# Moving two matmul operands by 192 bytes modulo 512 in a two-layer encoder kernel

## The chip, the core and the metric

The kernel runs on one core of a Trainium2 chip. The metric is device time in microseconds (us) of one execution; the time shown is the median of the runs taken, with the lowest and the highest beside it. A profile is one further execution, recorded instruction by instruction.

## What is computed

The reference is a two-layer encoder trunk over 256 tokens of width 2048, in float32. Each layer has an attention part (neighbourhood attention in the first layer, grouped-query attention in the second, both next to cross-attention into 256 memory tokens), an output projection, and a dense MLP with a hidden width of 8192:

```python
for i in range(DEPTH):                       # DEPTH = 2
    n = rms_norm(h, attn_norm[i])
    ...                                      # attention heads, cross-attention
    h = h + jnp.concatenate([mix, cross], axis=-1) @ w_o[i]
    n = rms_norm(h, mlp_norm[i])
    h = h + jnp.square(jax.nn.relu(n @ w_up[i])) @ w_down[i]
return rms_norm(h, final_norm)
```

The change touches the last matrix product of the MLP, with `w_down`.

## The kernel before

**Three products for one.** Matrix products run on TensorE in the type float32r. To keep float32 precision, each operand is split into a high part and a remainder (`split`: ScalarE copies the high part, VectorE subtracts it from the source), and a product is made as high x high, high x low and low x high. In the down product these three matmuls are the lines 1380, 1383 and 1384, in that order.

**A matmul has two operands.** The stationary operand (128 x 128, the weights of TensorE) is loaded first, by an instruction of its own, and the moving operand (128 rows of 256 or 512 columns, 4 bytes each) is then streamed through it. In the up product (`products`, line 419) the parts of `w_up` are stationary and the activations `hT` move, 256 columns at a time. In the down product (`down_grains`) the activations `a_s` are stationary and the parts of `w_down` move, 512 columns at a time.

**The MLP as a sequence of steps.** `add_mlp` writes one order by hand. After four leading up blocks it runs 60 steps per layer; a step is `down[0]`, `up[0]`, `up[1]`, `down[1]`:

- `down[0]` ("first"): nine matmuls with the parts `bh`, `bl` of three column blocks of `w_down`;
- `up[0]` and `up[1]`: 48 matmuls that make the next block of 128 hidden units, with the parts `uh`, `ul`. The first of them uses a separate copy of its weights, `u_0` (in the profile `u`);
- `down[1]` ("second"): twelve matmuls with the parts `th`, `tl` of four *combined* blocks, sums of column blocks that a Strassen scheme of seven products needs.

So twelve matmuls with `th`, `tl` follow the 48 of the up product in each step, and the nine with `bh`, `bl` of the next step follow them. Over both layers there are 120 steps. After the last step some plain down products remain (`plain_grains`); there the rooms of `th` and `tl` are used again for the parts `h_p`, `l_p` of a chunk's second half. In the leading up blocks one half uses the same rooms as `u_th`, `u_tl`.

**The order on the engines.** `run_all` runs the grains in this order and issues preparations a few grains ahead; matmuls of the steps are kept in program order (`pin`). The steps' parts are written by ScalarE (line 516, high part) and VectorE (line 517, remainder).

**Places.** Tiles lie one behind another in each partition of the on-chip memory, so the size of one sets where the next begins. Several constants of the kernel (`U_AT`, `MOVING_AT`, `LAST_AT`, `STILL_AT`, `COPY_AT` and others) shift a tile within a slightly larger room, so that it begins at a chosen byte address modulo 512. "Place" below means byte address modulo 512 in the partition. Worked out from the tile sizes and the order in which the pools stack them, the places in the steps are:

| operand | role | place before | place after |
|---|---|---|---|
| `hT`, chunks 0 to 14 | moving, 256 columns | 160 | 160 |
| `hT`, last chunk (k = 15) | moving, 256 columns | 384 | 384 |
| `uh`, `ul` (two buffers in turn) | stationary | 224 for `up[0]`, 480 for `up[1]` | same |
| `u` (copy of the first weights) | stationary | 352 | 352 |
| `a_s` (all its blocks) | stationary | 128 | 128 |
| `th`, `tl` | moving, 512 columns | 128 | 320 |
| `bh`, `bl` | moving, 512 columns | 128 | 128 |
| `u_th`, `u_tl` (leading up block) | stationary | 224 | 224 |
| `h_p`, `l_p` (plain products) | moving, 512 or 256 columns | 128 | 128 |

Of the kernel before, what the change touches and what calls it, by code (L numbers as in the profile page):

```python
# [11 lines left out]
F32R = mybir.dt.float32r  # L12
# [5 lines left out]
P = 128  # L18
# [15 lines left out]
CH = 2048  # L34
HALF = CH // 2
# [22 lines left out]
U_AT = 96  # L58
# [5 lines left out]
LONGER = {"hi": 128, "lo": 128}  # L64

COPY_AT = 384
MASKED = -1e30


# [95 lines left out]
def encoder_kernel(ctx: ExitStack, tc: tile.TileContext, t: dict, out: bass.AP):  # L165
# [56 lines left out]
    for q in range(4):  # L222
        s = slice(q * 512, (q + 1) * 512)
# [969 lines left out]
    def loaded(src, tag):  # L1193
        raw = at.side.tile([P, CH], F32, tag=tag, bufs=3 if tag == "b" else 2, name=f"raw_{tag}")
        nc.sync.dma_start(raw, src)
        return raw

    def up_grains(layer, m):
        own = {}
        lead = m < LEAD  # L1200

        def load():
            own["raw"] = loaded(t[f"w_up{layer}"][m], "U")

        def prep(hf):

            if m == 2:
                past(lambda: prepared(hf), box["splits"][-1])
                return
            if m == 3 and layer == 0:  # L1210
                past(lambda: prepared(hf), box["ready"])
                return
            if m in (LEAD, LEAD + 1):
                past(lambda: prepared(hf), box["both", m - LEAD])
                return
            if m == 1 and hf == 0 and layer == 0:
                past(lambda: prepared(hf), box["turns"])
                return
            with tc.issue_after(box["summed"].ins) if m == hf == 1 else nullcontext():
                prepared(hf)  # L1220

        def prepared(hf):
            half = 2 * m + hf
            if lead and half in (2, 4, 5, 6, 7):

                if half < 5:
                    room = at.side.tile([P, 2, HALF], F32R, tag="b", bufs=3, name="u_b")
                    own[hf] = room[:, 0], room[:, 1]
                elif half > 5:
                    room = at.mlp.tile([P, 2, HALF], F32R, tag=f"z{hf}", name="u_z")  # L1230
                    own[hf] = room[:, 0], room[:, 1]
                else:
                    s = slice(U_AT // 4, U_AT // 4 + HALF)
                    own[hf] = tuple(at.mlp.tile([P, CH], F32R, tag=x, name=f"u_{x}")[:, s] for x in ("th", "tl"))
                box["splits"].append(split(*own[hf], own["raw"][:, hf * HALF : (hf + 1) * HALF]))
            else:
                own[hf] = half_of_side(own["raw"], hf)
            if not lead and hf == 0:

                room = at.side.tile([P, 256], F32R, tag="junk", bufs=1, name="u_0")  # L1240
                own["first"] = room[:, COPY_AT // 4 :][:, :P]
                nc.scalar.activation(own["first"], own["raw"][:, :P], AF.Copy)

        def run(hf):
            if m == hf == 0:
                closed("cat", "ring")
                at.mlp = opened("mlp")

                last = at.mlp.tile([P, 14 * P], F32R, tag="a", bufs=6, name="hT_l")[:, LAST_COPY_AT // 4 :][:, :SEQ]
                nc.scalar.activation(last, box["hT"][:, KT - 1, :SEQ].bitcast(F32), AF.Copy)  # L1250
                box["hT0"] = Plain(box["hT"], last)
            if hf == 0:
                if lead:
                    pool, tag, bufs = (at.att, "att", at.banks) if m == 2 else (at.acc, "acc", None)
                    own["ps"] = pool.tile([P, 512], F32, tag=tag, bufs=bufs, name="ps_u")[:, :SEQ]
                else:
                    own["ps"] = sum_of("up")[:, :SEQ]

            acts = box["hT0" if lead else "hT"]
            if m < 3 and hf == 1:  # L1260
                hi, lo = own.pop(hf)
                last = products(own["ps"], acts, KT // 2, KT // 4, hi, lo)
                box.setdefault("rests", []).append((m, own["ps"], hi[:, HALF // 2 :], lo[:, HALF // 2 :]))
                if m == 2:
                    for other, ps, hi, lo in box.pop("rests"):
                        with tc.issue_after(last.ins):
                            last = products(ps, acts, KT * 3 // 4, KT // 4, hi, lo)
                        squared(layer, other, ps)
                return
            with tc.issue_after(box["late"].ins) if m == hf == 0 else nullcontext():  # L1270
                products(own["ps"], acts, hf * (KT // 2), KT // 2, *own.pop(hf),
                         keep_order=not lead, first=own.pop("first", None))

        def after():
            if m > 2:
                squared(layer, m, own["ps"])

        early = (8, 8, 6)
        return [Grain(lambda: run(0), None, load, None, lambda: prep(0), early if m < 2 else SOONER),
                Grain(lambda: run(1), after, None, None, lambda: prep(1), early if m == 0 else SOONER)]  # L1280
# [44 lines left out]
    def down_grains(layer, n, begins, ends, sooner):  # L1325

        q, j = STEPS[n]
        own = {}
# [32 lines left out]
                split(*own["first"], own["b"].rearrange("p a b -> p (a b)")[:, : 3 * 512])  # L1361

        def prep_second():
            own["second"] = tuple(at.mlp.tile([P, CH], F32R, tag=x, name=x) for x in ("th", "tl"))
            with tc.issue_after(box["relu"].ins) if n == 0 else nullcontext():
                split(*own["second"], own["t"].rearrange("p a b -> p (a b)"))

# [100 lines left out]
    def plain_grains(layer, nb, at_chunk):  # L1468

        last = layer == 1 and nb == REST[-1]  # L1470
        parted = layer == 1 and nb == REST[-2]
        w = Work("M", None, left_of, 0, True, True, None, finish if last else down_done(layer, nb))
        nc_ = len(chunks_left(nb))
        own = {}

        def load(c):
            own[c] = loaded(t[f"w_plain{layer}"][at_chunk + c], "Ub"[(at_chunk + c) % 2])

        def prep(c, hf):
            if (at_chunk + c) % 2 == 0:  # L1480
                own[c, hf] = half_of_side(own[c], hf, MOVING_AT)
            else:
                own[c, hf] = tuple(at.mlp.tile([P, HALF], F32R, tag="bt"[hf] + x, name=f"{x}_p") for x in "hl")
                box["rest"] = split(*own[c, hf], own[c][:, hf * HALF : (hf + 1) * HALF])


        PIECES = [(c, hf, ((UPS // 2 - min(STEPPED)) // 2 - nc_ + c) * 4 + hf * 2, 2) for c in range(nc_) for hf in range(2)]

        def begin():
            if nb == REST[0]:  # L1490
                closed("ps_sums")
                open_sums(layer)
            w.ps = [at.acc.tile([P, 512], F32, tag="acc", name="ps_m") for _ in range(NT)]
            if last:

                w.ps.append(at.acc.tile([P, 512], F32, tag="acc", name="ps_m"))

        def run(n):
            if last:
                return  # L1500
            c, hf, k0, nk = PIECES[n]
            if n == 0:
                begin()
            for i in range(1 if parted else NT):
                m_products(w, k0, nk, i, *own[c, hf], n == 0, n == len(PIECES) - 1)

        def second():
            for n, (c, hf, k0, nk) in enumerate(PIECES):
                m_products(w, k0, nk, 1, *own[c, hf], n == 0, n == len(PIECES) - 1, keep_order=True)
            tile_done(w, nb, 1)  # L1510

        def after():
            if parted:
                for i in range(NT):
                    first_shares(i)
                tile_done(w, nb, 0)
                tile_gf(nb, 0)
                box["second"] = second
                return
            if not last:  # L1520
                w.done(w)
                return

            begin()

            def products(i, bank, *part):
                for n, (c, hf, k0, nk) in enumerate(PIECES):
                    m_products(w, k0, nk, i, *own[c, hf], n == 0, n == len(PIECES) - 1, keep_order=True, part=part,
                               bank=bank)
                return w  # L1530

            w.done(products, lambda: tile_gf(REST[-2], 1), box["second"])

        return [Grain(lambda n=n: run(n), after if n == len(PIECES) - 1 else None,
                      (lambda c=c: load(c)) if hf == 0 else None, None, lambda c=c, hf=hf: prep(c, hf), SOON)
                for n, (c, hf, _, _) in enumerate(PIECES)]

# [479 lines left out]
```

## Time and profile before

| what | value |
|---|---|
| median of 3 runs | 1989.57 us (1988.87 to 1990.09) |
| profiled execution: span from the first to the last instruction | 1986.6 us |
| granted TensorE clock over the span | 0.999 of full speed |
| TensorE busy | 1976.8 us, 12852 matmuls |
| VectorE busy | 1744.0 us |
| ScalarE busy | 1451.0 us |
| mean share of the 16 DMA engines, in the windows view | 0.72 |

For the profiled execution the page gives the span and no total time of its own. The median of the runs is 2.97 us above that span; what lies around the span is in this difference.

The page gives groups of instructions by source line, engine, operation and tile names, with the count, the summed busy time and the mean duration of one. The duration of a matmul runs from its start to a modelled end, so it is longer than the distance to the next start (successive matmuls overlap); two groups of the same shape can still be compared with each other, and the distance between starts in the timeline gives the pace itself. The timeline shows starts in steps of 0.01 us; the trace behind it holds nanoseconds (ns).

### The profile page before, as it was taken

The page shows a single profiled execution, that of the slowest core. Times are in us where ns is not written, and L with a number is a line of the kernel's source. Part 1 is how long each engine was busy: PE and PEld are TensorE (multiplying, and loading weights), DVE is VectorE, ACT ScalarE, POOL GpSimd, SP SyncE. Part 2 cuts the span into 40 slices and gives each one's busy share as a digit, 9 for nine tenths or more (in the row PEclk, how much of TensorE's full clock was granted, in tenths as well). Part 3 has the DMA queues.
Part 4 walks back from the last instruction along what each step waited for, and adds up shares of the span by engine and source line. Part 5 has one row for each costly group of instructions (what it writes and reads, how often), then busy time and mean ns, then how long its engine had stood idle before and what let it go on. Part 6 is the DMA issues. An engine that isn't in the chain of part 4 may idle for free.

```text
span 1986.6 us, 33222 instructions
## 1 busy us (share of the span) xinstructions
PE 1976.8 (100%) x12852; PEld 1797.3 (90%) x12852; DVE 1744.0 (88%) x2132; ACT 1451.0 (73%) x2123; POOL 156.1 (8%) x209
## 2 busy tenths in 40 slices
PE   9999999999999999999999999999999999999998
PEld 8999999899999999999998888889999999999997
DVE  6777768799999999999999879789999999999997
ACT  6655555677887778777887666667788777877786
POOL 0000000000000000000001001001000000000001
PEclk9999999999999999999999999999999999999999
DMA  7856566777777777777778765668777777777775
GB/s 291 321 192 208 203 199 195 273 225 239 228 225 237 230 226 237 233 240 227 223 228 226 268 219 172 221 205 257 238 228 225 236 231 227 236 232 240 229 225 157
DMA packets 113950, 454.57 MB, mean 229 GB/s; under 512 B 19072, under 2 KB 43776, under 8 KB 66432
## 3 DMA queue, kind: packets, MB, share of 16 engines
q1 hardware_dynamic: 92320, 414.43, 61.0%
q0 software_dynamic: 21184, 37.50, 10.8%
q8 instruction: 101, 1.65, 0.3%
q10 hardware_dynamic: 288, 0.52, 0.1%
q14 instruction: 57, 0.47, 0.1%
HBM read 397.78 MB, written 4.19 MB: 202 GB/s over the span
## 4 chain that ended last, share of the span: by engine, by line
PE 98%; ACT 1%; DVE 1%; issue 0%; DMA 0%; SPq 0%; POOL 0%; DVEq 0%; POOLq 0%; ACTq 0%
PE ps_u L419 35%; PE p L1380 10%; PE p L1384 10%; PE p L1383 10%; PE ps_s L419 9%; PE ps_m L399 7%; PE ps_m L400 7%; PE ps_m L396 7%; DMA raw<-in_w_first 0%; PE sc_ps L612 0%; PE sc_ps L614 0%; PE sc_ps L613 0%; PE av L708 0%; PE av L709 0%; PE av L710 0%
## 5 line engine op out<-in xcount | busy, mean ns | idle before, releaser
L419 PE MATMUL ps_u<-hT,uh 128*128 128x256 f32 x3812 | 662.5, 276 | 0.0
L419 PEld LDWEIGHTS ps_u<-hT,uh 128*128 128x128 f32 x3812 | 578.7, 188 | 5.7
L419 PE MATMUL ps_u<-hT,ul 128*128 128x256 f32 x1964 | 542.6, 276 | 0.0
L516 ACT ACTIVATE uh<-raw_U 128x1024 fp32r<-128x1024 f32 x258 | 273.4, 1061 | 157.0 <-PE ps_u L419 155.0
L419 PEld LDWEIGHTS ps_u<-hT,ul 128*128 128x128 f32 x1964 | 368.7, 188 | 0.0
L516 ACT ACTIVATE hi<-raw 128x1024 fp32r<-128x1024 f32 (+2 forms) x215 | 221.0, 1032 | 161.3 <-PE ps_m L400 78.3
L517 DVE TENSOR_TENSOR lo<-raw,hi 128x1024 fp32r<-128x1024 f32 (+2 forms) x215 | 253.4, 1185 | 86.6 <-ACT hi L516 86.1
L517 DVE TENSOR_TENSOR ul<-raw_U,uh 128x1024 fp32r<-128x1024 f32 x258 | 314.1, 1219 | 11.6 <-ACT uh L516 11.6
L517 DVE TENSOR_TENSOR tl<-t,th 128x2048 fp32r<-128x2048 f32 x120 | 274.7, 2290 | 51.7 <-ACT th L516 51.3
L516 ACT ACTIVATE th<-t 128x2048 fp32r<-128x2048 f32 x120 | 230.9, 1924 | 92.5 <-PE p L1384 92.5
L517 DVE TENSOR_TENSOR bl<-b,bh 128x1536 fp32r<-128x1536 f32 x120 | 210.2, 1752 | 0.3 <-ACT bh L516 0.3
L1348 POOL DMA_DIRECT2D t<-b x120 | 103.4, 862 | 1175.6 <-ACT t L1347 1090.6
L1380 PE MATMUL p<-th,a_s 128*128 128x512 f32 x480 | 187.5, 391 | 0.0
L1383 PE MATMUL p<-tl,a_s 128*128 128x512 f32 x480 | 187.2, 390 | 0.0
L1384 PE MATMUL p<-th,a_s 128*128 128x512 f32 x480 | 186.7, 389 | 0.0
L516 ACT ACTIVATE bh<-b 128x1536 fp32r<-128x1536 f32 x120 | 178.7, 1489 | 3.5
L419 PE MATMUL ps_s<-nT,hi 128*128 128x256 f32 x896 | 154.6, 277 | 0.0
L1384 PE MATMUL p<-bh,a_s 128*128 128x512 f32 x360 | 140.9, 391 | 0.0
L1383 PE MATMUL p<-bl,a_s 128*128 128x512 f32 x360 | 140.1, 389 | 0.0
L1380 PE MATMUL p<-bh,a_s 128*128 128x512 f32 x360 | 140.1, 389 | 0.0
L419 PEld LDWEIGHTS ps_s<-nT,hi 128*128 128x128 f32 x896 | 135.3, 188 | 0.2
L419 PE MATMUL ps_s<-nT,lo 128*128 128x256 f32 x448 | 124.2, 277 | 0.0
(343 smaller groups left out, 3715.4 us busy)
## 6 DMA issues: line engine op xcount, KB each, us to landing
raw_U<-in_w_up SPq DMA_DIRECT2D x128, 1024.0 KB, 6.4
b<-in_w_pair SPq DMA_DIRECT2D x120, 1024.0 KB, 5.8
raw<-in_w_o SPq DMA_DIRECT2D x32, 1024.0 KB, 5.0
t<-b POOLq DMA_DIRECT2D x120, 256.0 KB, 6.6
raw<-in_w_b SPq DMA_DIRECT2D x21, 1024.0 KB, 5.6
raw<-in_w_av SPq DMA_DIRECT2D x12, 1024.0 KB, 5.0
raw<-in_w_aq SPq DMA_DIRECT2D x12, 1024.0 KB, 5.0
raw<-in_w_ak SPq DMA_DIRECT2D x12, 1024.0 KB, 4.9
```

Of the source, the lines that this page charges most:

```text
L396: first = nc.tensor.matmul(ps, ah, hi[:, s], start=st, stop=False)
L399: nc.tensor.matmul(ps, ah, lo[:, s], start=False, stop=False)
L400: final = nc.tensor.matmul(ps, al, hi[:, s], start=False, stop=sp)
L419: ins = nc.tensor.matmul(ps, x, acts[:, k, part], start=k == n == 0, stop=k == KT - 1 and n == 2)
L516: first = nc.scalar.activation(dst_hi, src, AF.Copy)
L517: return first, nc.vector.tensor_tensor(dst_lo, src, dst_hi.bitcast(F32), op=ALU.subtract)
L1348: nc.gpsimd.dma_start(s[:, 3, :], b[:, 1, :], accum_op=ALU.add)
L1380: ins = nc.tensor.matmul(ps, a[:, 0, ai, :], hi[:, s], start=entered, stop=False, skip_group_check=True)
L1383: nc.tensor.matmul(ps, a[:, 0, ai, :], lo[:, s], start=False, stop=False, skip_group_check=True)
L1384: nc.tensor.matmul(ps, a[:, 1, ai, :], hi[:, s], start=False, stop=ends, skip_group_check=True)
```

## The change

The tiles `th` and `tl` get larger rooms: 192 bytes more for `th`, 320 bytes more for `tl`, together 512, so that every tile behind them keeps its place. In `down[1]` the parts begin 192 bytes into `th`'s room and at the start of `tl`'s room, which itself begins 192 bytes later than before. Both end up at place 320. The two other users of the rooms are shifted back, so that they keep their places. No instruction is added, removed or reordered, and no shape changes.

```diff
+T_AT = {"th": 192, "tl": 0}
+T_LONGER = {"th": 192, "tl": 320}
...
+    def t_room(tag, name):
+        return at.mlp.tile([P, CH + T_LONGER[tag] // 4], F32R, tag=tag, name=name)
+
     def up_grains(layer, m):
...
                 else:
-                    s = slice(U_AT // 4, U_AT // 4 + HALF)
-                    own[hf] = tuple(at.mlp.tile([P, CH], F32R, tag=x, name=f"u_{x}")[:, s] for x in ("th", "tl"))
+                    own[hf] = tuple(t_room(x, f"u_{x}")[:, (U_AT + as_before) // 4 :][:, :HALF]
+                                    for x, as_before in (("th", 0), ("tl", 320)))
...
         def prep_second():
-            own["second"] = tuple(at.mlp.tile([P, CH], F32R, tag=x, name=x) for x in ("th", "tl"))
+            own["second"] = tuple(t_room(x, x)[:, T_AT[x] // 4 :][:, :CH] for x in ("th", "tl"))
...
             else:
-                own[c, hf] = tuple(at.mlp.tile([P, HALF], F32R, tag="bt"[hf] + x, name=f"{x}_p") for x in "hl")
+                if hf:
+                    own[c, hf] = t_room("th", "h_p")[:, :HALF], t_room("tl", "l_p")[:, 320 // 4 :][:, :HALF]
+                else:
+                    own[c, hf] = tuple(at.mlp.tile([P, HALF], F32R, tag="b" + x, name=f"{x}_p") for x in "hl")
```

## The prediction

> **What bounds the kernel now.** I read the page first: span, busy times, and the chain that ended last.
>
> ```profile
> span 1986.6 us, 33222 instructions
> ...
> PE 1976.8 (100%) x12852; PEld 1797.3 (90%) x12852; DVE 1744.0 (88%) x2132; ACT 1451.0 (73%) x2123; POOL 156.1 (8%) x209
> ...
> PE 98%; ACT 1%; DVE 1%; issue 0%; DMA 0%; SPq 0%; POOL 0%; DVEq 0%; POOLq 0%; ACTq 0%
> ```
>
> TensorE (PE) is the chain. Then the view of waits, for TensorE alone; these are all its rows:
>
> ```profile
> PE idle L245 <- POOL mhalf L239: 1.0, 1, 1.0
> PE ps_s L419 <- ACT hi L516: 0.5, 1, 0.5
> ```
>
> In the steps TensorE waits for no other engine. What is left is its own pace: does each matmul start as early as it can after the one before? For that I read the timeline of TensorE around one step (start in us first), with the entry of two other steps, and one weight load:
>
> ```profile
> 457.71 0.40 PE L1380 MATMUL p<-th,a_s 128*128 128x512 f32 x1
> ...
> 1005.06 0.28 PE L419 MATMUL ps_u<-hT,ul 128*128 128x256 f32 x1
> ...
> 1009.48 0.28 PE L419 MATMUL ps_u<-hT,ul 128*128 128x256 f32 x1
> ...
> 1009.95 0.40 PE L1380 MATMUL p<-th,a_s 128*128 128x512 f32 x1
> 1010.18 0.39 PE L1383 MATMUL p<-tl,a_s 128*128 128x512 f32 x1
> 1010.41 0.39 PE L1384 MATMUL p<-th,a_s 128*128 128x512 f32 x1
> ...
> 1014.49 0.40 PE L1384 MATMUL p<-bh,a_s 128*128 128x512 f32 x1
> ...
> 1050.85 0.40 PE L1380 MATMUL p<-th,a_s 128*128 128x512 f32 x1
> ```
>
> ```profile
> 1010.18 0.19 PEld L1384 LDWEIGHTS p<-th,a_s 128*128 128x128 f32 x1
> ```
>
> Undisturbed pace, 512 columns: from 1010.41 to 1014.49 lie 18 matmuls, 4.08 us, 226.7 ns each. 256 columns: from 1005.06 to 1009.48 lie 39, 4.42 us, 113.3 ns each. A step without any disturbance would take 48 x 113.3 + 21 x 226.7 = 10200 ns. The first `th` matmuls of two steps that lie 58 steps apart start at 457.71 and 1050.85: 593.14 / 58 = 10226.6 ns. So 27 ns of a step, 3.2 us over 120 steps, are disturbance. This is the most that any placement in the steps can give back: 0.16% of the time.
>
> The loads show when two operands are read together: the weights of the next matmul are loaded from the moment the present one starts (the load for the matmul at 1010.41 starts at 1010.18, with the matmul before it). So the pair that matters is the moving operand of one matmul and the stationary operand of the next. I call *distance* the place of the latter less the place of the former, modulo 512.
>
> **Do places matter at all?** In the groups kept apart by shape, similar matmuls at other places have other durations (mean ns behind the comma):
>
> ```profile
> L419 PE MATMUL ps_u<-hT,u 128*128 128x256 f32 x120 | 33.0, 275 | 0.0
> ...
> L419 PE MATMUL ps_u<-hT,u_b 128*128 128x256 f32 x96 | 11.9, 276 | 0.0
> L419 PE MATMUL ps_u<-hT,u_z 128*128 128x256 f32 x92 | 11.1, 279 | 0.0
> ...
> L396 PE MATMUL ps_m<-h_p,a_p 128*128 128x512 f32 x28 | 10.9, 389 | 0.0
> ...
> L613 PE MATMUL sc_ps<-km,qmT 128*128 128x256 f32 x16 | 4.5, 282 | 0.0
> ...
> L396 PE MATMUL ps_m<-h_p,a_p 128*128 128x256 f32 x8 | 2.3, 282 | 0.0
> ```
>
> `u_b` and `u_z` are weights of the same product, with the same `hT` at 160. `u_b` lies at 480 (distance 320): 276 ns, as all undisturbed ones of 256 columns. `u_z` lies at 128 (distance 480): 279. `km` and `qmT` both lie at 480 (distance 0): 282. `h_p` against `a_p` has distance 0: 282 with 256 columns, but an undisturbed 389 with 512. So at 256 columns distance 320 is clean and 0 costs 6 ns each time; at 512 columns 0 is clean. No row has 512 columns at distance 320, which is what the change makes.
>
> By the Trainium skill (SBUF — State Buffer, Who interferes with whom) PE has independent read ports for moving operand and weights and never waits on anyone; by that the change gives nothing and the time stays 1989.6 us. The 276 and 279 of `u_b` and `u_z` disagree with it.
>
> **The change part by part.** No instruction, transfer, wait or order changes. Four things can move.
>
> *1. The entry into `th`, `tl`.* Page, groups (ACT and DVE rows serve part 4):
>
> ```profile
> L517 DVE TENSOR_TENSOR ul<-raw_U,uh 128x1024 fp32r<-128x1024 f32 x258 | 314.1, 1219 | 11.6 <-ACT uh L516 11.6
> L517 DVE TENSOR_TENSOR tl<-t,th 128x2048 fp32r<-128x2048 f32 x120 | 274.7, 2290 | 51.7 <-ACT th L516 51.3
> L516 ACT ACTIVATE th<-t 128x2048 fp32r<-128x2048 f32 x120 | 230.9, 1924 | 92.5 <-PE p L1384 92.5
> ...
> L1380 PE MATMUL p<-th,a_s 128*128 128x512 f32 x480 | 187.5, 391 | 0.0
> L1383 PE MATMUL p<-tl,a_s 128*128 128x512 f32 x480 | 187.2, 390 | 0.0
> L1384 PE MATMUL p<-th,a_s 128*128 128x512 f32 x480 | 186.7, 389 | 0.0
> ...
> L1384 PE MATMUL p<-bh,a_s 128*128 128x512 f32 x360 | 140.9, 391 | 0.0
> ...
> L1380 PE MATMUL p<-bh,a_s 128*128 128x512 f32 x360 | 140.1, 389 | 0.0
> ```
>
> Line 1384 is clean (186.7 us for 480). Line 1380 has 0.8 us more and line 1383 0.5 us more, over the same 480. It sits in the first two matmuls of each step, as view by tile shows of line 1380 (shortest, median, longest):
>
> ```profile
> L1380 PE MATMUL p<-th,a_s x480: 389/389/396, 447.5 to 1955.7; 128*128 128x512 f32 x160
> ```
>
> The median is 389, the longest 396; 0.8 us / 120 entries = 7 ns, which is the whole difference between median and longest. So each entry costs 7 + 4 = 11 ns, 1.3 us over 120. These two matmuls come out of a disturbed stretch (the last `hT` chunk lies at 384, not 160), and at distance 0 they need two matmuls until the pace is back. After the change they are at distance 320. Ends: nothing is saved (0), or all of it (-1.3 us), or the entry grows; the nearest row for growth is in part 2. I take -1.3 us, because 320 is clean with 256 columns, the stricter case: there a load must fit into 113.3 ns, here it has 226.7. And for the first 256 columns the two reads are the same as there.
>
> *2. The seam from `th` to `bh`.* Now distance 0 follows 0; after the change 0 follows 320. Two seams of the trace bound it, one from distance 256 at 512 columns to 320 at 256, and one into 512 columns out of a run at 320:
>
> ```profile
> 213.44 0.28 PE L419 MATMUL ps_s<-nT,lo 128*128 128x256 f32 x1
> ...
> 214.00 0.28 PE L419 MATMUL ps_s<-nT,lo 128*128 128x256 f32 x1
> ```
>
> ```profile
> 190.53 0.40 PE L396 MATMUL ps_m<-hi,nT 128*128 128x512 f32 x1
> ...
> 191.69 0.39 PE L400 MATMUL ps_m<-hi,nT 128*128 128x512 f32 x1
> ```
>
> In the first the five matmuls from 213.44 on take 0.56 us, 5 x 113.3 = 0.567: free. In the second the five from 190.53 on take 1.16 us, 5 x 226.7 = 1.133: 27 ns lost. It has a change of width and a load that just fits before it; the seam `th` to `bh` has neither, all 512 columns, so it is nearer to the free one. I take 0; ends 0 and +27 ns x 120 = +3.2 us.
>
> *3. The ten other matmuls of `down[1]`.* All twelve, 1440 in total, now stand at distance 320. Clean: 0. If 320 is wrong for 512 columns, each pays what a wrong distance pays in the rows above, 3 ns (`u_z`) to 6 ns (`km`), so +4.3 to +8.6 us; the one disturbed matmul of 512 columns that recurs (last `bh` before `u`, line 1384: 0.8 us / 120 = 7 ns) gives +9.6. I take 0, as in part 1.
>
> *4. Writes, and the shifted users.* ScalarE and VectorE write `th`, `tl` at place 320. `ul` at 224 or 480 takes 1219 ns for 1024 columns; the remainder of the same size at place 128 (view by tile) takes a median of 1218:
>
> ```profile
> L517 DVE TENSOR_TENSOR l_p<-raw_b,h_p x8: 1211/1218/1222, 1048.5 to 1969.0; 128x1024 fp32r<-128x1024 f32 x8
> ```
>
> So the place costs VectorE nothing visible. Even 1% of 2290 ns, 23 ns a step, would be covered: over the 58 steps VectorE is busy 552.70 of 593.14 us (third time in the row):
>
> ```profile
> 457.71:1050.85 593.14, 593.14 (x4004) 544.69 (x4003) 552.70 (x567) 473.04 (x610) 51.33 (x61) 1.00 0.75 231
> ```
>
> That leaves 0.7 us a step. If this cover were gone, 23 ns x 120 = 2.8 us would show, as waits of TensorE for `tl`. ScalarE sits idle 92.5 us before `th`. `u_th`, `u_tl`, `h_p`, `l_p` keep their places: 0. The exit from `bh` to `u` (0.8 us) and the last `hT` chunk of each step keep both their places: 0.
>
> Sum: -1.3 us. The span of the profiled execution goes from 1986.6 to 1985.3 us. The median of the runs lies 2.97 us above the span, and I leave that as it is: 1989.57 - 1.3 = 1988.3 us.
>
> **The rivals.**
>
> - *Nothing changes* (1989.6 us). The 11 ns belong to the change from 256 to 512 columns out of a disturbed stretch, and two matmuls are needed whatever the place. For it: the seam at 190.53 also loses on the way into 512 columns. Against it: `bh` to `u` changes width too, and there the first matmul of 256 columns (`u`, 275 ns) is clean at once.
> - *The loss moves on* (1991.5 us). The entry is clean, but the seam to `bh`, now from 320 to 0, loses the 27 ns of 190.53: +16 ns net a step, +1.9 us. For it: there, too, a run at distance 320 lay ahead. Against it: the free seam at 213.44.
> - *Slower: 320 is wrong at 512 columns* (1993.9 to 1999.2 us, middle 1996). It decides from 2.8 ns a matmul on (4.0 us / 1440). For it: distance 0 is clean at 512 and not at 256 columns, so the clean distances of the two widths differ. Against it: the difference is explained if a delayed load is hidden at 512 and not at 256, and by that what is clean at 256 is clean at 512.
> - *Faster by more than 0.2%*: the whole 3.2 us of disturbance is less than that.
>
> **How the numbers follow.** 0.2% is 4.0 us, about what a measurement of this kernel can tell from no change. Chances: forecast 0.52, nothing changes 0.17, the loss moves on 0.16, slower 0.14, faster 0.01. The first three are all within 0.2%: 0.85. The range for 8 in 10 takes these three: below, the full 1.3 us and the 0.7 us that the runs of before lie apart downwards, 1987.6; above, the loss that moves on with 0.5 us of the same scatter, 1992.0. The forecast's own range is 1987.6 to 1988.9.
>
> **What would show it.** Step right: lines 1380 and 1383 of `th`, `tl` fall to the 186.7 us of line 1384, the longest of line 1380 falls from 396 to about 389, and the first `th` of steps 58 apart lie 593.14 - 58 x 0.011 = 592.5 us apart. Nothing changes: 396 stays. Loss moves on: line 1380 or 1383 of `bh`, `bl` of the page rises above the 140.1 us of line 1380. Slower: line 1384 of `th` rises above 186.7, with its median over 389. The prediction would be wrong above all if distance 320 disturbs every matmul of 512 columns, or if VectorE became late for `tl`, which the view of waits would name.

## The result and the profile after

| kernel | median | runs | span of the profiled execution |
|---|---|---|---|
| before | 1989.57 us (1987.60 to 1990.09) | 5 | 1986.6 us |
| after | 2000.79 us (1998.98 to 2001.64) | 5 | 1999.0 us |

The ratio after to before is 1.0057, 95% interval 1.0046 to 1.0068: 11.2 us slower, where 1988.3 us was predicted. The time is nearest to the rival "320 is wrong at 512 columns", 1.6 us above that rival's upper end.

The view of TensorE's waits, all its rows after the change (engine, line, what ended the wait; us, times, longest). The change adds lines, so 419 has become 422, 516 and 517 are 519 and 520, and 1380, 1383, 1384 are 1386, 1389, 1390:

```profile
PE sc_ps L594 <- DVE kT L520: 1.5, 1, 1.5
PE idle L248 <- POOL mhalf L242: 1.0, 1, 1.0
```

No wait has come into the steps. The 1.5 us belong to the attention part, outside them: the first step starts 1.0 us later than before (448.48 against 447.46 us), which is most of the 1.2 us by which the profiled spans differ more (12.4 us) than the medians (11.2). In the steps TensorE waits for no other engine, as before, and some matmuls take longer. The groups by shape (mean ns behind the comma):

```profile
L520 DVE TENSOR_TENSOR tl<-t,th 128x2048 fp32r<-128x2048 f32 x120 | 274.7, 2289 | 58.5 <-ACT th L519 58.3
...
L1386 PE MATMUL p<-th,a_s 128*128 128x512 f32 x480 | 190.3, 396 | 0.0
L1389 PE MATMUL p<-tl,a_s 128*128 128x512 f32 x480 | 189.8, 395 | 0.0
L1390 PE MATMUL p<-th,a_s 128*128 128x512 f32 x480 | 189.8, 395 | 0.0
...
L1390 PE MATMUL p<-bh,a_s 128*128 128x512 f32 x360 | 141.3, 393 | 0.0
L1386 PE MATMUL p<-bh,a_s 128*128 128x512 f32 x360 | 141.1, 392 | 0.0
L1389 PE MATMUL p<-bl,a_s 128*128 128x512 f32 x360 | 140.8, 391 | 0.0
```

The three groups of `th`, `tl`, which had 389 to 391 ns, now have 395 to 396, and `bh`, `bl`, which were not moved, went up too. VectorE's `tl` is unchanged (2290 before). The view by tile gives the shortest, median and longest of a line, here the third matmul line of `th` before and after:

```profile
L1384 PE MATMUL p<-th,a_s x480: 389/389/389, 447.9 to 1956.1; 128*128 128x512 f32 x160
```

```profile
L1390 PE MATMUL p<-th,a_s x480: 393/394/398, 448.9 to 1968.4; 128*128 128x512 f32 x160
```

Before, all three were 389. Now the shortest is 393: not one of these matmuls ran undisturbed. The timeline shows what that costs in pace (start in us first):

```profile
458.80 0.40 PE L1386 MATMUL p<-th,a_s 128*128 128x512 f32 x1
...
461.60 0.40 PE L1386 MATMUL p<-bh,a_s 128*128 128x512 f32 x1
...
1057.36 0.40 PE L1386 MATMUL p<-th,a_s 128*128 128x512 f32 x1
```

The twelve matmuls take 2.80 us where 12 x 226.7 = 2.72 would do. A step takes (1057.36 - 458.80) / 58 = 10320 ns, before 10227: 93 ns more, and 120 x 93.4 ns = 11.2 us is the whole difference of the medians.

To see where in a step the 93 ns lie, I take from the nanosecond starts in the trace the *excess* of each matmul: its start to the next start, less 226.7 ns (512 columns) or 113.3 ns (256), averaged over the steps.

| matmuls of a step | excess before | excess after |
|---|---|---|
| last `uh`, `ul` | 4.2, 5.0 | the same |
| twelve `th`, `tl` | 5.9, 4.2, then 0 | 7.5, 9.2, then 4.2 and 9.1 by turns to the end |
| their sum | 10 | 83 |
| nine `bh`, `bl` | 0; last one (before `u`) 8.2 | 9.9, 5.8, 4.1, then 0; last one 8.2 |

So +73 ns in `th`, `tl` and +20 ns in `bh`, `bl`.

### The profile page after: what moved, and what is told of

It is laid out like the page before. It is cut to its first block, busy times and chain, and to the rows that moved or that the text cites. A ratio compares the mean times of both kernels' runs of the same rounds, so it can differ in the third digit from the quotient of the medians.

```text
span 1999.0 us, 33222 instructions
## 1 busy us (share of the span) xinstructions
PE 1988.2 (99%) x12852; PEld 1798.1 (90%) x12852; DVE 1746.6 (87%) x2132; ACT 1451.7 (73%) x2123; POOL 157.6 (8%) x209
## 4 chain that ended last, share of the span: by engine, by line
PE 97%; DVE 1%; issue 1%; ACT 1%; DMA 0%; POOL 0%; DVEq 0%; POOLq 0%; ACTq 0%
PE ps_u L422 35%; PE p L1386 10%; PE p L1390 10%; PE p L1389 10%; PE ps_s L422 9%; PE ps_m L402 7%; PE ps_m L403 7%; PE ps_m L399 7%; DMA c_x<-cat 0%; DVE nT L550 0%; PE sc_ps L617 0%; PE sc_ps L616 0%; PE sc_ps L615 0%; PE av L711 0%; PE av L712 0%
## 5 line engine op out<-in xcount | busy, mean ns | idle before, releaser
L520 DVE TENSOR_TENSOR tl<-t,th 128x2048 fp32r<-128x2048 f32 x120 | 274.7, 2289 | 58.5 <-ACT th L519 58.3
L1386 PE MATMUL p<-th,a_s 128*128 128x512 f32 x480 | 190.3, 396 | 0.0
L1389 PE MATMUL p<-tl,a_s 128*128 128x512 f32 x480 | 189.8, 395 | 0.0
L1390 PE MATMUL p<-th,a_s 128*128 128x512 f32 x480 | 189.8, 395 | 0.0
```

The lines of the kernel that those rows point to most:

```text
L520: return first, nc.vector.tensor_tensor(dst_lo, src, dst_hi.bitcast(F32), op=ALU.subtract)
L1386: ins = nc.tensor.matmul(ps, a[:, 0, ai, :], hi[:, s], start=entered, stop=False, skip_group_check=True)
L1389: nc.tensor.matmul(ps, a[:, 0, ai, :], lo[:, s], start=False, stop=False, skip_group_check=True)
L1390: nc.tensor.matmul(ps, a[:, 1, ai, :], hi[:, s], start=False, stop=ends, skip_group_check=True)
```

## The experiments

Three theories stood at first: *width* (each width has its own clean distances; at 512 columns 320 is not one), *entry* (320 is clean, but a run that is entered disturbed stays so) and *place* (the absolute place 320 is bad); in the expectations they are called W, L and P. Each time is compared with runs of the kernel before that were taken beside it, whose medians lie between 1988.05 and 1989.95 us. Periods are those of a step, the mean from the trace: 10226.9 ns before, 10320.1 after. A run or stage is *clean* where the excess is 0, and the *entry* is the change from the up stage to `th`, `tl`, the *exit* that from `bh`, `bl` to `u`.

### A sweep of distances

The shape of the kernel after, with `th`, `tl` at another place each step (16-byte steps over 256 bytes), and the copy of `u` in 32-byte steps over 512:

```diff
-            own["second"] = tuple(t_room(x, x)[:, T_AT[x] // 4 :][:, :CH] for x in ("th", "tl"))
+            own["second"] = tuple(t_room(x, x)[:, 16 * (n % 16) // 4 :][:, :CH] for x in ("th", "tl"))
...
-                own["first"] = room[:, COPY_AT // 4 :][:, :P]
+                own["first"] = room[:, 32 * ((m - LEAD + (m - LEAD) // 16) % 16) // 4 :][:, :P]
```

> Both rooms of th and tl are 256 bytes longer and the parts begin 16 x (n mod 16) bytes into them in step n, so that one run holds all distances in 16-byte steps over 256 bytes (0 to 240 below zero, modulo 256); the copy u moves in 32-byte steps as well, independently of it. Theory W (which distance is clean depends on the width: at 512 columns 0 modulo 256, at 256 columns 64): the eight steps with offset 0 stand at 389 ns after their entry, those with offset 192 (distance 64 modulo 256, as in the changed kernel) at 395, the others also above 389; in all about 15/16 of the 11.2 us, 2000 us. Theory L (320 is clean in itself, but at 512 columns a run that is entered disturbed gets stuck): several of the 16 offsets stand at 389, time 1992 to 1997 us. Theory P (place 320 of the moving operand is bad at 512 columns whatever the weights): only offset 192 is above 389, about 1/16 to 1/8 of 11.2 us, 1990 to 1991 us. Exit from bh to u: 8 ns at the place 352 now; 0 is expected where u lies at 128 or 384 (distance 0 or 256).

Measured: 2012.08 us in one run, more than any theory gave; the up stages below are why. Excess of the twelve `th`, `tl` together, by distance: at 0 it is 10 to 28 ns, and the last five of the twelve have none (the run comes back to the pace); each of the other fifteen stays disturbed to the end, with 45 to 119 ns, and 320 has 83 to 85 whatever ran ahead of it. So 0 is the only one of the sixteen swept that comes back within twelve matmuls at 512 columns. Only 0 and 272 to 496 were swept. The distance 256 is clean at 512 columns too, in rows of the kernel before (`ps_m` from `hi` and `nT`, shown under part 2 below).

The copy of `u` brought what I had not looked for. The 48 matmuls of the up stage are the same in each step, at the same distances but for the copy. Two such stages, from `u` to the first `th`; in the first pair the copy lies at 64, in the second at 352 as in the kernel before:

```profile
472.47 0.28 PE L422 MATMUL ps_u<-hT,u 128*128 128x256 f32 x1
...
478.13 0.39 PE L1386 MATMUL p<-th,a_s 128*128 128x512 f32 x1
...
566.74 0.28 PE L422 MATMUL ps_u<-hT,u 128*128 128x256 f32 x1
...
572.18 0.40 PE L1386 MATMUL p<-th,a_s 128*128 128x512 f32 x1
```

5.66 against 5.44 us (48 x 113.3 = 5.44). In the slow stages all 48 matmuls are some 4.4 ns late each, 213 ns a stage; 70 of the 118 stages between two steps of this run are slow. With 256 columns at distance 64 or 320 there are two lasting paces, and the way in picks one. The place of the copy is not the whole of the way in here, since `th`, `tl` ahead differ too (a copy at 96 or 416 stands before stages of either pace); a later sweep moves the copy alone.

### Everything at 320, at distance 0

From the kernel before: the whole pool, `a_s` too, begins 192 bytes further on.

```diff
                 at.mlp = opened("mlp")
+                at.mlp.tile([P, 192 // 4], F32, tag="pad", name="pad")
```

> The kernel before with one pad of 192 bytes ahead of all tiles of the MLP's pool: th, tl, bh, bl and a_s all lie at 320, so that every distance inside the down products is 0 again. Theory W and theory L: the down products are clean (median 389), only the entry and the exit change: 1988 to 1993 us. Theory P: all 2520 matmuls of 512 columns at place 320 pay about 7 ns: +17 us, 2006 us.

Measured: 1997.67 us (1997.47 to 1998.58), ratio 1.0046 (1.0029 to 1.0063).

```profile
L1384 PE MATMUL p<-bl,a_s 128*128 128x512 f32 x360 | 140.1, 389 | 0.0
L1381 PE MATMUL p<-bh,a_s 128*128 128x512 f32 x360 | 140.1, 389 | 0.0
```

`bh`, `bl` at place 320, written there by ScalarE and VectorE as `th`, `tl` are after the change, run at their old 389 ns and 140.1 us. The place theory falls: 320 as such costs nothing. The time is nevertheless above the 1988 to 1993 us of the other two theories. The step takes 10300.0 ns: 22 ns more than before are lost in the first matmuls of the up stage, and 51 ns at the entry, since the moving operand of the last `ul` matmul now stands at another distance from `a_s`. The twelve `th`, `tl` need ten matmuls to come back (excess 14.2, 8.3, 6.7, 9.2, -2.5, 4.2, 9.2, 1.7, 5.9, 4.2, 0, 0; sum 61 ns). Even at distance 0 the entry sets how long recovery takes.

### The twelve matmuls as 24 of 256 columns

Each `th`, `tl` matmul is written as two halves, once at 320 (from the kernel after) and once at 128 (from the kernel before):

```diff
-                nc.tensor.matmul(ps, a[:, 0, ai, :], lo[:, s], start=False, stop=False, skip_group_check=True)
...
+                halves = [slice(0, 512)] if which == "first" else [slice(0, 256), slice(256, 512)]
+                for part, x, st, sp in ((0, hi, entered, False), (0, lo, False, False), (1, hi, False, ends)):
+                    for c in halves:
+                        pin(nc.tensor.matmul(ps[:, c], a[:, part, ai, :], x[:, s][:, c], start=st and c.start == 0,
+                                             stop=sp and c.stop == 512, skip_group_check=True))
```

At 320:

> The changed kernel with each of the 1440 matmuls of th and tl made as two of 256 columns (the weights loaded for each). Theory W: 256 columns at distance 320 are clean, as in the up product: the loss is gone, 1987.5 to 1990.5 us. Theory L: the run is entered as disturbed as before and stays so: 2000 us or more. Theory P: the same place, 2 x 1440 x 3 to 7 ns: 1998 to 2010 us.

At 128:

> The kernel before (th and tl at 128, distance 0) with the same halves of 256 columns. Theory W: distance 0 is clean at 512 columns alone; 2880 matmuls pay about 6 ns: +17 us, 2007 us. Theories L and P: place 128 stays clean: 1989 to 1991 us.

Measured: 2005.22 us (ratio 1.0083, 1.0068 to 1.0098) and 2009.18 us (1.0101, 1.0086 to 1.0116). The groups at 320, then at 128:

```profile
L1389 PE MATMUL p<-th,a_s 128*128 128x256 f32 x1920 | 323.8, 281 | 0.0
```

```profile
L1383 PE MATMUL p<-th,a_s 128*128 128x256 f32 x1920 | 327.0, 282 | 0.0
```

At 128 each half is 6.7 ns late from the seventh on, near the 6 ns that the row of `km` had; this is what the width theory expected (2007 us), and against the other two. At 320 each is 4.1 to 4.9 ns late (the first 3.4), the slow pace of the up stage, although the row of `u_b` shows 320 clean at this width; here the width theory expected no loss. So it falls in its simple form too: a clean row at 256 columns tells of a distance *and* of how the run was entered.

### 320 at 512 columns, entered clean

This separates what is left of width and entry at 512 columns. From the kernel before: `bh`, `bl` at 320, `th`, `tl` back at 128.

```diff
+B_LONGER = {"bh": 192, "bl": 320}
...
-            own["first"] = tuple(at.mlp.tile([P, 3 * 512], F32R, tag=x, name=x) for x in ("bh", "bl"))
+            own["first"] = tuple(b_room(x, x, at_byte, 3 * 512) for x, at_byte in (("bh", 192), ("bl", 0)))
```

> Mirror image of the change: the combined halves bh, bl of down[0] begin at place 320, th and tl stay at 128 as before. So 9 matmuls of 512 columns a step (1080 in all) stand at distance 320, and they are entered from th at distance 0, which has come back to its clean pace by then. Theory 'only 0 is clean at 512 columns': each of the nine pays 4 to 9 ns whatever ran ahead of it, some 60 ns a step, +7 us, so 1996 to 1998 us. Theory 'the change only kept a disturbed entry alive': entered clean, 320 stays clean, 0 ns, 1989 to 1990 us. Beside both: the place of the last bh against the copy of u is now 32 away and no longer 224, so the 48 matmuls of the following up stage may run at their slow steady state (about 205 ns a step more, +25 us); that part is read off the up stage alone and not counted for either theory.

Measured: 1996.61 us (1996.35 to 1997.12), ratio 1.0040 (1.0025 to 1.0054).

```profile
L1388 PE MATMUL p<-th,a_s 128*128 128x512 f32 x480 | 186.9, 389 | 0.0
...
L1388 PE MATMUL p<-bh,a_s 128*128 128x512 f32 x360 | 142.3, 395 | 0.0
L1384 PE MATMUL p<-bh,a_s 128*128 128x512 f32 x360 | 142.0, 394 | 0.0
L1387 PE MATMUL p<-bl,a_s 128*128 128x512 f32 x360 | 141.9, 394 | 0.0
```

```profile
L1384 PE MATMUL p<-bh,a_s x360: 393/394/398, 440.1 to 1955.4; 128*128 128x512 f32 x180
```

`th` has its 389 again, and the ten `th`, `tl` ahead of `bh` have an excess of 0. Nevertheless the first `bh` already has 6.6 ns, and each of the nine has 6.5 to 6.8, 60 ns in all (the ninth, with the copy of `u` as its next weights, included); the shortest of the line is 393. The entry theory falls for 512 columns: 320 is disturbed from the first matmul on. The copy of `u` did not throw the up stage into its slow pace (14 ns in its first four matmuls, then 0). Period 10293.3 ns; 120 x 66.4 = 8.0 us, measured 7.7.

### One part of the change alone

From the kernel after: `th` stays at 320, `tl` goes back to 128.

```diff
-T_AT = {"th": 192, "tl": 0}
+T_AT = {"th": 192, "tl": 320}
```

> One part of the change alone: th at place 320 (distance 320), tl back at 128 (distance 0). Of the twelve matmuls of down[1], eight have th and four tl, in the order th, tl, th. Theory 'each matmul pays for its own distance': the eight at 320 pay some 6.7 ns and the four at 0 nothing, 54 ns a step against 83 after the change, so some 1996.5 us. Theory 'a disturbed run is a state, and only a run of clean matmuls ends it': one tl between two th is too short, all twelve pay, and bh still needs its three matmuls: 1999 to 2001 us. Were th at 320 harmless and tl the cause, 1989.5 us.

Measured: 2003.77 us (2003.55 to 2004.50), ratio 1.0076 (1.0061 to 1.0091): half of the change costs more than the whole, and more than any theory gave.

```profile
L1389 PE MATMUL p<-tl,a_s 128*128 128x512 f32 x480 | 191.5, 399 | 0.0
L1386 PE MATMUL p<-th,a_s 128*128 128x512 f32 x480 | 191.0, 398 | 0.0
L1390 PE MATMUL p<-th,a_s 128*128 128x512 f32 x480 | 188.5, 393 | 0.0
...
L1390 PE MATMUL p<-bh,a_s 128*128 128x512 f32 x360 | 142.5, 396 | 0.0
```

The four `tl`, at distance 0, are the slowest (12.4, 10.0, 12.5, 10.0 ns), and `bh`, `bl` do not come back within nine matmuls (44 ns). So a matmul does not pay for its own distance alone: its delay depends on those before it, and one matmul at distance 0 between others at 320 does not bring the pace back.

### All seams at distances that had shown clean

From the kernel before: the pool 96 bytes further on (`a_s`, `th`, `tl`, `bh`, `bl` all at 224), the last `hT` chunk at 160 in layer 0 and 416 in layer 1, the copy of `u` at 480 and 224 by turns.

```diff
-LAST_AT = 224
+LAST_AT = (0, 256)
...
-                own["first"] = room[:, COPY_AT // 4 :][:, :P]
+                own["first"] = room[:, (256, 0)[m % 2] // 4 :][:, :P]
...
+                at.mlp.tile([P, 96 // 4], F32, tag="pad", name="pad")
```

> Every seam of a step at a distance that has shown itself clean: mlp tiles at 224 (distance 0 at 512 columns throughout), the last hT chunk so that ul to a_s is 64, uh to ul 64 or 320, and the copy of u at 224 or 480 by turns so that bh to u is 0 or 256. If distances of 64 modulo 256 at 256 columns and 0 at 512 are clean whenever entered clean, the 27 ns of disturbance a step go: up to -3.2 us, 1986.4 to 1988 us. If a change of width costs by itself, nothing goes: 1989.5 us. If one seam throws the up stage into its slow steady state (4.4 ns a matmul, 213 ns a step), up to 2015 us, and the step at which it begins names the seam.

Measured: 2010.69 us (2010.06 to 2011.14), ratio 1.0110 (1.0094 to 1.0125), the case of the slow up stage.

```profile
L419 PE MATMUL ps_u<-hT,uh 128*128 128x256 f32 x3812 | 686.2, 281 | 0.0
...
L1385 PE MATMUL p<-th,a_s 128*128 128x512 f32 x480 | 186.9, 389 | 0.0
L1384 PE MATMUL p<-tl,a_s 128*128 128x512 f32 x480 | 186.9, 389 | 0.0
L1381 PE MATMUL p<-th,a_s 128*128 128x512 f32 x480 | 186.9, 389 | 0.0
```

All 21 matmuls of 512 columns are clean, the entry and the last `bh` included, and the whole up stage runs slow: `uh` 281 ns against 276, 213 ns a step. The first matmul after the exit, `u`, is already 4.1 ns late, and nothing after it recovers.

On this kernel I swept the copy of `u` alone:

```diff
-                own["first"] = room[:, (256, 0)[m % 2] // 4 :][:, :P]
+                own["first"] = room[:, 32 * (m % 16) // 4 :][:, :P]
```

> A look at the seam that the last run left over. Base is the kernel of e10 (the combined tiles and a_s all at place 224, distance 0 throughout, which there ran without any disturbance at 512 columns); only the copy of u, the weights loaded during the last bh of a step, stands at another place each step, in 32-byte steps over 512 bytes. Theory 'the distance from bh to the copy decides': with bh 96 bytes further, the places that were clean against bh at 128 (distances 224, 256 and 0) are clean again, so copies at 448, 480 and 224; but 224 and 480 ran slow in e10. Theory 'the absolute place of the copy against hT decides': 352, 384 and 128 are clean again whatever bh's place. Theory 'after a bh at 224 the up stage is always slow': all sixteen show some 210 ns a step, and the time is that of e10, 2010 to 2012 us. With half of the places clean, some 2000 us.

Measured: 1999.88 us in one run. Two up stages, with the copy at 448 (distance 224 from `bh`) and at 480 (distance 256):

```profile
556.59 0.28 PE L419 MATMUL ps_u<-hT,u 128*128 128x256 f32 x1
...
562.03 0.39 PE L1381 MATMUL p<-th,a_s 128*128 128x512 f32 x1
...
566.81 0.28 PE L419 MATMUL ps_u<-hT,u 128*128 128x256 f32 x1
...
572.46 0.39 PE L1381 MATMUL p<-th,a_s 128*128 128x512 f32 x1
```

5.44 against 5.65 us. Ten of the sixteen places give a clean stage, six a slow one; 192 and 448 are best (8.3 ns at the last `bh`, 3 to 4 behind it). Distance 224 from `bh` is clean with `bh` at 128 (the copy at 352 in the first sweep) and with `bh` at 224; 0 and 256, clean with `bh` at 128, are slow here. None of the theories held: neither distance nor place alone decides. And after a clean up stage `th`, `tl` have 15 ns, after a slow one 45 ns (copy at 64, 128, 320, 384) or none (224, 480). With the best copy, at 448, a step loses 26.5 ns, where the kernel before loses 26.9.

### The entry, by the last chunk of hT

From the kernel before, `LAST_AT` given for each layer: `(0, 160)`, then `(128, 192)` and `(288, 96)`, which puts the last chunk at 160 and 320, at 288 and 352, at 448 and 256.

> From the kernel before: only the last chunk of hT moves, to place 160 in layer 0 and 320 in layer 1 (384 before, in both), so the last uh and ul of a step stand at another distance from the a_s that is loaded during them; th and tl stay at distance 0. Theory 'distance 0 comes back to the clean pace, and the entry sets only how long that takes': the steps of the two layers differ from each other in the excess of the first matmuls of th and tl, between 0 and some 60 ns a step, with bh clean in both; 1988 to 1994 us in all. Theory 'the entry costs a fixed 11 ns for the change of width': no difference between the layers, 1989.5 us.

> From the kernel before, as in the run with the last hT chunk at 160 and 320: the last chunk of hT now at place 288 in layer 0 and 352 in layer 1. Seen so far a step (whole disturbance): 27 ns at 384, 47 at 320, 73 at 160. Theory 'only the distance of the last ul to a_s counts' (here 352 and 288): no case yet at these, 27 to 75 ns each. Theory 'the entry can be made free': one of the places gives 8 ns a step (the exit alone), which for one layer is -1.1 us. Expected sum over both layers 1988.5 to 1994 us.

> The same with the last chunk of hT at place 448 in layer 0 and 256 in layer 1 (distances of the last ul to a_s 192 and 384). Theory 'the entry can be made free': 8 ns a step in one of the layers; otherwise 27 to 75 ns a step. Expected 1988.5 to 1994 us.

Measured: 1992.67 us (ratio 1.0021, 1.0012 to 1.0030), 1991.28 us and 1991.59 us (one run each). Step periods from the trace, less 10200 ns:

| last chunk at | 160 | 256 | 288 | 320 | 352 | 384 (before) | 448 |
|---|---|---|---|---|---|---|---|
| ns over 10200 | 72.5 | 40.0 | 13.3 | 46.8 | 46.7 | 26.9 | 46.7 |

`th`, `tl` stay at distance 0 and come back in each case, and the entry sets how soon; it is not a fixed 11 ns for the change of width, since the layers of one run differ (72.5 against 46.8 ns). With 288 the twelve have 0.8 ns together, and the disturbance of a step is halved, so I ran it in both layers:

```diff
-LAST_AT = 224
+LAST_AT = 128
```

> The kernel before with the last chunk of hT at place 288 in both layers (384 before), nothing else. By the accounting of the steps, a step keeps 13.4 ns of disturbance (5.0 in the last uh, 8.2 at the exit to u) instead of 26.6, so 120 x 13.3 ns = 1.6 us less, ratio 0.9992. If the accounting misses something between the steps, ratio 1.000. A measurement of five rounds may not tell these two apart by time alone; the distance between the first th matmuls of steps 58 apart does: 58 x 10213.4 = 592.38 us against 593.14.

Measured: 1987.39 us (1986.32 to 1988.68, 11 runs) against 1988.82 (1987.88 to 1991.62, 15 runs), ratio 0.9990 (0.9981 to 0.9999).

```profile
1361.46 0.39 PE L1380 MATMUL p<-th,a_s 128*128 128x512 f32 x1
...
1953.84 0.39 PE L1380 MATMUL p<-th,a_s 128*128 128x512 f32 x1
```

58 steps take 592.38 us, before 593.14: 13 ns a step, 1.6 us over 120, where the medians differ by 1.43. It is the fastest of all kernels here, but by less than the 0.2% that the prediction took as the least that a measurement tells from no change; the step period is the firmer evidence.

## Why the prediction was wrong, by its steps

**The reading of the bound was right.** TensorE's own pace was the limit and operand places moved it; waits did not. The nine changed kernels with more than one run, the one after among them, all differ from the kernel before by what 120 steps of their period give, within 0.7 us.

**Parts 1 and 3, one inference.** Both took 320 as clean at 512 columns because it was clean at 256, "the stricter case". That is the step that failed, and the prediction had named it as what would break it. The row behind it (`u_b`, 276 ns) showed a state that the way in had picked: the same distance at the same width also runs 4 to 5 ns late for good (the halves at 320, the slow up stages). And 512 columns behave in another way: of the sixteen distances swept only 0 comes back, and 320 is late from the first matmul even out of a clean run (`bh`, `bl` at 320: 6.6 ns each). Nor had "stricter" a row behind it. It rested on a load that must fit into 113.3 ns, but the loads of the up stage in the profile before last longer than that:

```profile
L419 PEld LDWEIGHTS ps_u<-hT,uh 128*128 128x128 f32 x3812 | 578.7, 188 | 5.7
```

Part 1, at -1.3 us, measured (7.5 + 9.2 - 5.9 - 4.2) x 120 = +0.8 us. Part 3, at 0, measured 66.6 ns x 120 = +8.0 us for the ten others. Its other end, +4.3 to +9.6 us, was worked out for all twelve matmuls, and all twelve measured 0.8 + 8.0 = 8.8 us, inside it.

**Part 2, the seam to `bh`.** At 0 with an upper end of 27 ns; measured 9.9 + 5.8 + 4.1 = 19.8 ns, +2.4 us. It had dismissed the seam at 190.53, where 27 ns are lost, for the free one at 213.44. The run ahead of the free one was clean, as the timeline of before shows:

```profile
211.17 0.39 PE L400 MATMUL ps_m<-hi,nT 128*128 128x512 f32 x1
...
213.21 0.39 PE L400 MATMUL ps_m<-hi,nT 128*128 128x512 f32 x1
```

Nine matmuls in 2.04 us, 9 x 226.7 = 2.04, at distance 256. The run of `th`, `tl` at 320 is not clean, and `bh` behind it begins late, although in the kernel before the same `bh`, `bl` run at 0 behind a clean run. The five matmuls from 190.53 on have an excess of 6.3, 9.3, 1.3, 6.3 and 3.3 ns and then 0.3, a recovery over several matmuls like those of the experiments. The three parts add up: 0.8 + 8.0 + 2.4 = 11.2 us, the difference measured.

**The rivals.** "Slower: 320 is wrong at 512 columns" happened, and with the sign that it named (the third line of `th` rose from 186.7 to 189.8 us, its median to 394 ns). Its price for the twelve matmuls held (8.8 us in 4.3 to 9.6), but it did not add the seam of part 2, 2.4 us, which the same disturbance brings with it: 1999.2 us at the most, 2000.8 measured. "The loss moves on" and this rival were thus not alternatives but two terms of one sum. Its chance of 0.14 was too low, for the page held evidence of another rule at 512 columns (0 clean there, not at 256) that was explained away by an argument about hidden loads, with no row behind it.

**Part 4 was right.** VectorE's `tl` took 2289 ns (2290 before), and in the window of 58 steps it is busy 553.70 of 598.56 us (the third time in the row):

```profile
458.80:1057.36 598.56, 598.56 (x4005) 544.83 (x4003) 553.70 (x566) 474.05 (x610) 51.34 (x61) 1.00 0.75 229
```

The granted clock, 1.00 in that window as before, has no part in it either.

**Two independent ports.** By the Trainium skill ("SBUF — State Buffer", Who interferes with whom), TensorE's two read ports are independent and it waits for nothing. The runs disagree: with no wait for another engine in the trace, the pace of matmuls depended on the places of the moving operands and of the weights loaded meanwhile. The mean excess of one matmul of a step lay between -2.5 and 14.2 ns, both in the run with everything at 320.

**What stays open.** Why a run at 512 columns comes back at distance 0 (and at 256, in the rows from 190.53 on) and at none of the other fifteen swept, and what picks between the two paces at 256 columns: the sweeps show that the delays depend on the matmuls before, but no run here shows the mechanism behind that.

## What to carry to other kernels

A group of like durations may show a state that the way in has set, not a property of its operands: before a clean row is carried to another shape or another neighbour, look for the same pair of operands running late elsewhere. Where delays depend on what ran before, changes of single seams do not add up; price the whole step, and sweep places in one kernel (a place for each step or layer), which reads a dozen cases from one trace. And when two rivals share their cause, their prices belong in one sum.

## What the hardware showed that was not expected

- At 256 columns and distance 64 or 320, 48 identical matmuls ran at 113.3 ns each or at some 4.4 ns more, to the end of the stage, decided, in the sweep of the copy alone, by the place of a single load before them (5.44 or 5.65 us a stage).
- At 512 columns `th`, `tl` at distance 320, entered disturbed, settle into a fixed alternation, 4.2 and 9.1 ns; `bh`, `bl` at 320, entered clean, have 6.5 to 6.8 ns each, the same mean. A matmul at distance 0 between two at 320 is later still, 10.0 to 12.5 ns.
- Recoveries at distance 0 end on one sequence. Within 0.3 ns the excess runs 9.2, 1.7, 5.8, 4.2, 0 with everything at 320, with the last chunk of `hT` at 160, 256, 320, 352 and 448, and in `bh` behind the halves at 128; a shorter one shows its end alone (9.9, 5.8, 4.1, 0 after the change). The entry seems to set only where on this path a run begins; no run was made to test that.
- Single matmuls started up to 2.5 ns sooner than 226.7 ns after the one before within a recovery (-2.5 ns, in the pool shifted as a whole), so a part of the delay is given back.
- A slow up stage could be left without loss (0 ns in the twelve `th`, `tl` behind it, with the copy at 224 or 480), where each clean stage of the same kernel cost 15 ns.
